# A two-layer hybrid decoder trunk on one core: the order of issue in five places, and a last product in one step

## The chip, the cores and the metric

The kernel runs on one core of one Trainium2 chip. The metric is the device time of one execution in microseconds (us): the median of several runs. A profile is taken of one further execution; its times count from the first instruction of that execution, and its span ends with the last.

## The reference

A trunk of two layers works on x, 512 positions by 1024 channels, in float32. Each layer is half a SwiGLU block (1024 to 2 x 2816, back to 1024), a token mixer, and half a SwiGLU block again, each behind an RMS norm and added to x. The mixer of layer 0 is recurrent, that of layer 1 a gated unit in chunks of 128 positions. A norm with a gain ends it.

```
h = h + 0.5 * swiglu(rms_norm(h, g1), w_in, w_out)
m = recurrent_mixer(hn) or spatial_gating_mixer(hn)
h = h + m
h = h + 0.5 * swiglu(rms_norm(h, g2), w_in, w_out)

recurrent:  y, r = split(hn @ w_in);  r = causal_conv4(r)
            gate_a, gate_x = sigmoid(block_diagonal(r))
            a = exp(-8 * gate_a * softplus(-lam));  b = r * gate_x * sqrt(1 - a*a)
            s[t] = a[t] * s[t-1] + b[t];  m = (gelu(y) * s) @ w_out
gating:     u, v = split(gelu(hn @ w_in));  v = rms_norm(v)
            m = (u * (tril(w_s) @ v + b_s)) @ w_out
```

## The kernel before

All matrix products run on TensorE in the type fp32r with three matmuls for one: an operand is split into a rounded part hi and the rest lo, and hi*hi, lo*hi and hi*lo are summed in one PSUM bank. ScalarE makes hi by a copy, VectorE makes lo by a subtraction (`split`, line 95). Weights are split the same way (whi, wlo, `Sub.split`, line 164). x stays in SBUF for the whole run.

Most products follow a scheme of Strassen's kind: a two by two block product in seven products (`seven`, line 312), named P1, P2, P5, P6, P3, P7, Q4. Their left operands are the quarters A11, A12, A22 and A21 of the activations and the sums S1 to S4 of them; their results are gathered in the PSUM banks A, B, C and, in the output products, Q. A result is put together when the last K slice of a product is done (the functions p1 to q4, the "posts").

The order of all work is written out by hand. `subs` is a list of steps; a step is one weight block (up to 128 x 1024 elements) and the matmuls that use it. The loop at line 1303 walks the list: at step i it runs what was hooked to the step's phase "pre", splits the weights of the steps up to i + 3 (`ahead` sets other numbers for the first steps), runs phase "mid", starts loads, issues the matmuls of step i and with them the posts, and runs the phases "end" and "late". `hook(n, phase, fn)` puts work there. Each engine carries out its instructions in the order of issue, so a hook's place decides what stands behind what on that engine. Weights come through eight raw buffers, loaded on SyncE's queue; accumulating loads go over GpSimd's. There are four buffers each for whi and wlo, so the split for step i + 3 waits for the matmuls of step i - 1. PSUM has six banks for products and two ("aux") for transposes.

The places that the change touches:

- **Opening** (lines 1259 to 1301). The first SwiGLU block begins before the first norm is known: the rows' factor is applied after the product. x is transposed by TensorE in quarters (`turn`), evacuated with the gains by ScalarE (`take`), and the first six steps (`pair_plain`, line 654) use A12, A11, S1 and A22 in two groups of 256 channels. Squares, mean, square root and Newton's step (`squares`, `rstd`) give the rows' factor.
- **Decay constants** (`lru_consts`, line 1152): softplus of lambda on 128 x 8 values, a chain of tiny VectorE operations, drawn at steps 24 to 44 a few at a time.
- **Norm before the recurrent mixer** (`TileNorm`, line 456). For two halves of 256 positions: squares, root, scaled rows xn (`rows`), 16 transposes into four banks (`turn`; two blocks of 128 channels to a bank), and then z as zh (ScalarE) and zl (VectorE) for the eight blocks k = 0 to 7 (`take`). The r and y products sum over these k (`mk`, line 928).
- **Recurrence** (`recurrent`, line 789). Steps 0 to 11 make the eight channel blocks of r: each is evacuated with the first tap of the convolution (rc, ScalarE), gets three more taps (VectorE), is split, goes through the gate matmuls and through two sigmoids and a tanh. Steps 12 to 19 make the eight blocks of y. `plan` (line 902) places for each block the exp and square, oma2 (1 + a squared, times tanh), sqrt, the scan, gelu and the product yh; `drain` moves a y block out of PSUM. The output product begins at step 20.
- **Gating mixer** (`seven_chunk`, line 993): `soon` places gelu and square of v behind the posts p2, p3 and p7.
- **Final norm** (`FinalNorm`, line 730). Tiles 0 and 1 are complete before P7, tiles 2 and 3 with Q4; `mean`, `root`, `newton`, `grown` (times the gain) and `store` write them out.

Of the kernel before, what the change touches and what calls it, by code (L numbers as in the profile page):

```python
# [10 lines left out]
AF = mybir.ActivationFunctionType  # L11
# [5 lines left out]
H = T // 2  # L17
# [16 lines left out]
SLOTS = 60  # L34

# [14 lines left out]
def trunk(ctx: ExitStack, tc: tile.TileContext, a: dict, out: bass.AP):  # L50
# [261 lines left out]
    def seven(block, cuts, left, w, posts, order=None, own=False, apart=False):  # L312
# [4 lines left out]
        bk, raw = {}, {}  # L317
        banks = dict(BANK, Q4=("Q", True)) if apart else BANK

        def mm_of(prod, ci):  # L320
# [3 lines left out]
            def mm(sub):  # L324
                for s in range(2):
                    if fresh and ci == 0:
                        bk[name, s] = bank(name)[:, :w]
                    ps = bk[name, s]
                    k = {} if fresh else dict(skip_group_check=True)
                    for q, i in enumerate(pairs):  # L330
                        zh, zl = left(prod, i, s)
                        wh, wl = sub.hi[:, q, :], sub.lo[:, q, :]
                        end = ci == len(cuts) - 1 and q == len(pairs) - 1
                        nc.tensor.matmul(ps, zh, wh, start=fresh and ci == 0 and q == 0, stop=False, **k)  # L334
# [84 lines left out]
    class BlockNorm:  # L419
# [21 lines left out]
        def rest(self, n, a22=4):  # L441

            for i, g in enumerate(self.g):
                hook(n + (9 if self.plain else a22), "mid", lambda g=g: g.parts("A22"))
# [11 lines left out]
    class TileNorm:  # L456
# [29 lines left out]
        def take(self, half):  # L486
            for k in range(KD):
# [9 lines left out]
        def quarter(self, name):  # L497
            n = now[0]
            last = name == "A21"
            squares(n + 1, "pre" if last else "mid", name)  # L500
            if name == "A12":
                rstd(n, (2, "pre"), (2, "mid"), (3, "pre"), cols=slice(0, 2))
                hook(n + 3, "mid", lambda: self.rows(0))
                hook(n + 3, "end", self.turn)
                hook(n + 4, "mid", lambda: self.take(0))
            elif last:
                S.z = self.z
                rstd(n, (1, "mid"), (1, "mid"), (2, "pre"), cols=slice(2, 4), new=False)
                hook(n + 2, "pre", lambda: self.rows(2))
                hook(n + 2, "end", self.turn)  # L510
                hook(n + 3, "mid", lambda: self.take(1))


    def out_blocks(w, k0, groups, scale, norm=None, order=None, own=False):
# [46 lines left out]
        def q4(s, ps):  # L561
            if hasattr(norm, "last"):
# [7 lines left out]
                      dict(P1=p1, P2=p2, P5=p5, P6=p6, P3=p3, P7=p7, Q4=q4), order, own, True)  # L570
# [83 lines left out]
    def pair_plain(w_in, f0, group, first=False):  # L654
# [24 lines left out]
        def post(half):  # L679
# [6 lines left out]
            left_blocks(group, ht, half, 2)  # L686
# [3 lines left out]
        for h in range(2):  # L690
            subs.append(Sub(raw[0, h], lambda sub, h=h: (product(sub, 0, "A11", h, False, h == 1),
                                                         product(sub, 1, "S1", h, h == 0, False)),
                            None if h == 0 else (lambda: hook(now[0] + 2, "late", lambda: post(0))) if first else
# [36 lines left out]
    class FinalNorm:  # L730
# [40 lines left out]
        def piece(self, t, n):  # L771
            at = now[0]
            hook(at + 1, "mid", lambda: self.mean(t, n))
            if n == 1:
                hook(at + 2, "mid", lambda: self.grown(t, n))
            if t < 2 and n == 1:
# [568 lines left out]
```

## Time and profile before

| what | value |
|---|---|
| median of 3 runs | 1676.83 us (1674.86 to 1677.48) |
| the profiled execution | 1675.16 us, span 1673.5 us |
| TensorE busy | 1627.8 us (97%) |
| VectorE busy | 1374.7 us (82%) |
| ScalarE busy | 1036.1 us (62%) |
| TensorE clock granted, mean | 0.993 of full |

The page gives the busy time of each engine. Further views are used: the waits (who waited for whom: total in us, how often, the longest), windows (for a stretch: length, then busy time and instructions of PE, PEld, DVE, ACT, POOL, then the granted clock of TensorE, the share of the DMA engines and GB/s; a view for one tile shows that tile's instructions alone), and the timeline (start in us, duration in us, engine, line, operation, output <- inputs, shape, how many merged; in brackets the engine's idle time before it and what ended it). PE is TensorE, PEld its weight loads, DVE VectorE, ACT ScalarE, POOL GpSimd, SP SyncE. Of the tiles' names, whi and wlo are split weights, hi and lo split activations, e transposes of activations, p the banks of the first steps, xt and xn those of the norm, r, gate, rc, g, tl, h those of the recurrence, c the parts of v, junk the thrown-away output of a square, ss and ssq its sums, lc the decay constants, raw a weight as loaded.

### The profile page before, as it was taken

How to read it: one execution, taken by the hardware profiler on the slowest of the kernel's cores; microseconds unless marked ns; L12 is line 12 of the kernel's file. 1: busy time of each engine (PE TensorE's matmuls, PEld its weight loads, DVE VectorE, ACT ScalarE, POOL GpSimd, SP SyncE). 2: the span in 40 equal slices, each digit the busy share in tenths (PEclk: the TensorE clock that was granted, in tenths of full speed). 3: DMA queues.
4: the chain of work that ended last, by engine and by line, in shares of the span. 5: the costliest groups of instructions: out<-in, count | busy, mean ns of one | idle time of the engine just before them, and what ended most of it. 6: DMA issues, size and time to landing. Idle time of an engine off the chain costs nothing.

```text
span 1673.5 us, 20804 instructions
## 1 busy us (share of the span) xinstructions
PE 1627.8 (97%) x7477; PEld 1336.2 (80%) x7477; DVE 1374.7 (82%) x1820; ACT 1036.1 (62%) x1487; POOL 210.6 (13%) x191
## 2 busy tenths in 40 slices
PE   7999999989989999999999999999999999999996
PEld 5778888868868878888888788888778887888885
DVE  4898797776698897787888977878965988779778
ACT  6646556666847656556676565566864765565655
POOL 1111111200010111111101111111200011111110
PEclk9999999999999999999999999999999999999998
DMA  6676966952344767876837668768854557686682
GB/s 203 137 174 166 218 161 152 215 150 76 101 106 121 160 176 168 202 171 152 214 119 166 176 162 204 175 154 212 219 159 111 131 124 199 154 211 159 160 208 78
DMA packets 160712, 271.97 MB, mean 163 GB/s; under 512 B 11248, under 2 KB 37472, under 8 KB 160608
## 3 DMA queue, kind: packets, MB, share of 16 engines
q1 hardware_dynamic: 113392, 181.95, 35.3%
q0 software_dynamic: 44992, 86.06, 30.8%
q10 hardware_dynamic: 2224, 2.63, 0.5%
q8 instruction: 59, 0.97, 0.2%
q14 instruction: 45, 0.37, 0.1%
HBM read 268.50 MB, written 2.10 MB: 162 GB/s over the span
## 4 chain that ended last, share of the span: by engine, by line
PE 85%; DVE 9%; ACT 3%; issue 2%; DMA 1%; SPq 0%; ACTq 0%; DVEq 0%
PE A L335 13%; PE A L336 13%; PE A L334 13%; PE C L335 7%; PE C L334 7%; PE C L336 7%; PE e L254 3%; PE B L334 3%; PE B L336 3%; PE B L335 3%; DVE wlo L84 2%; PE p L676 1%; PE p L677 1%; PE p L675 1%; DVE x L90 1%
## 5 line engine op out<-in xcount | busy, mean ns | idle before, releaser
L84 DVE TENSOR_TENSOR wlo<-raw,whi 128x1024 fp32r<-128x1024 f32 (+1 forms) x538 | 640.1, 1192 | 223.8 <-ACT whi L93 223.2
L93 ACT ACTIVATE whi<-raw 128x1024 fp32r<-128x1024 f32 (+1 forms) x538 | 556.1, 1035 | 426.7 <-PE A L335 114.3
L335 PE MATMUL A<-whi,lo 128*128 128x512 f32 x984 | 386.2, 392 | 8.8 <-DVE lo L84 8.6
L334 PE MATMUL A<-whi,hi 128*128 128x512 f32 x984 | 392.4, 399 | 2.1 <-ACT c L93 2.1
L336 PE MATMUL A<-wlo,hi 128*128 128x512 f32 x984 | 384.9, 391 | 0.0
L335 PEld LDWEIGHTS A<-whi,lo 128*128 128x128 f32 x984 | 185.4, 188 | 51.1 <-DVE lo L84 15.1
L336 PEld LDWEIGHTS A<-wlo,hi 128*128 128x128 f32 x984 | 185.2, 188 | 39.9
L334 PEld LDWEIGHTS A<-whi,hi 128*128 128x128 f32 x984 | 185.1, 188 | 39.1 <-ACT c L93 2.6
L335 PE MATMUL C<-whi,lo 128*128 128x512 f32 x544 | 212.3, 390 | 0.7 <-DVE lo L84 0.5
L334 PE MATMUL C<-whi,hi 128*128 128x512 f32 x544 | 212.4, 390 | 0.0
L336 PE MATMUL C<-wlo,hi 128*128 128x512 f32 x544 | 211.8, 389 | 0.0
L131 POOL DMA_DIRECT2D raw<-in_ffn_w_in_dram x80 | 96.4, 1205 | 772.3 <-DVE raw L84 444.9
L84 DVE TENSOR_TENSOR raw<-raw,raw 128x1024 f32<-128x1024 f32 (+1 forms) x118 | 141.5, 1199 | 0.5
L84 DVE TENSOR_TENSOR lo<-a,hi 128x512 fp32r<-128x512 f32 (+1 forms) x196 | 127.2, 658 | 9.5 <-ACT hi L93 9.1
L131 POOL DMA_DIRECT2D raw<-in_ffn_w_out_dram x72 | 83.0, 1153 | 380.2 <-DVE wlo L84 141.3
L93 ACT ACTIVATE hi<-a 128x512 fp32r<-128x512 f32 (+1 forms) x196 | 116.8, 601 | 22.6 <-DVE a L84 20.2
L335 PEld LDWEIGHTS C<-whi,lo 128*128 128x128 f32 x544 | 102.3, 188 | 23.4 <-DVE lo L84 2.2
L336 PEld LDWEIGHTS C<-wlo,hi 128*128 128x128 f32 x544 | 102.3, 188 | 21.2
L334 PEld LDWEIGHTS C<-whi,hi 128*128 128x128 f32 x544 | 102.3, 188 | 21.2
L334 PE MATMUL B<-whi,hi 128*128 128x512 f32 x272 | 109.6, 403 | 0.0
L335 PE MATMUL B<-whi,lo 128*128 128x512 f32 x272 | 106.7, 392 | 1.9 <-DVE lo L84 1.9
L336 PE MATMUL B<-wlo,hi 128*128 128x512 f32 x272 | 106.7, 392 | 0.0
(162 smaller groups left out, 2156.9 us busy)
## 6 DMA issues: line engine op xcount, KB each, us to landing
raw<-in_ffn_w_in_dram SPq DMA_DIRECT2D x160, 512.0 KB, 4.3
raw<-in_ffn_w_out_dram SPq DMA_DIRECT2D x100, 512.0 KB, 5.4
raw<-in_ffn_w_in_dram POOLq DMA_DIRECT2D x80, 512.0 KB, 7.5
raw<-in_ffn_w_out_dram POOLq DMA_DIRECT2D x60, 512.0 KB, 7.8
raw<-in_sg_w_in_dram SPq DMA_DIRECT2D x18, 512.0 KB, 4.8
raw<-in_ffn_w_in_dram SPq DMA_DIRECT2D x32, 256.0 KB, 3.9
raw<-in_rec_w_in_dram SPq DMA_DIRECT2D x16, 512.0 KB, 4.1
raw<-in_ffn_w_out_dram SPq DMA_DIRECT2D x20, 256.0 KB, 4.7
```

The lines of the kernel that those rows point to most:

```text
L84: nc.vector.tensor_tensor(out=o, in0=x, in1=y, op=op)
L90: nc.vector.scalar_tensor_tensor(out=o, in0=x, scalar=s, in1=y, op0=op0, op1=op1)
L93: nc.scalar.activation(out=o, in_=x, func=f, **k)
L131: nc.gpsimd.dma_start(out=self.v, in_=src, accum_op=ALU.add)
L254: nc.tensor.transpose(ps[:, o : o + P], src(q, s), ident)
L334: nc.tensor.matmul(ps, zh, wh, start=fresh and ci == 0 and q == 0, stop=False, **k)
L335: nc.tensor.matmul(ps, zl, wh, start=False, stop=False, **k)
L336: nc.tensor.matmul(ps, zh, wl, start=False, stop=end, **k)
L675: nc.tensor.matmul(ps, zh, wh, start=start and q == 0, stop=False)
L676: nc.tensor.matmul(ps, zl, wh, start=False, stop=False)
L677: nc.tensor.matmul(ps, zh, wl, start=False, stop=stop and q == 1)
```

## The change

The loop gets a phase "rest" between "mid" and the loads. Then:

- Opening: the weights of steps 2 to 6 are split later or in another order; A22 is evacuated by VectorE (`take_plain`) instead of ScalarE; both S1 splits go into step 2's "pre" and both A22 splits into step 3's; the rows' factor is finished at step 4's "pre"; the first gated rows are placed one step earlier for the first half, and their transposes one step later for the second.
- Decay constants: one operation per step, at steps 24 to 100.
- Norm before the recurrent mixer: squares, root, rows and first transposes one phase to one step earlier, a square root of one element to load its table early, and k in the order 0, 2, 4, 6, 1, 3, 5, 7 in `take` and in the products.
- Recurrence: another plan; the exps of blocks 0 to 4 are issued in the step of r block 7, scans from step 14 on instead of 16.
- Gating mixer: gelu and square one to two steps later than before.
- Final norm: other phases; the stores of tiles 0 and 1 at the end; in the last Q4 the matmuls of both K slices are issued together, tile by tile.

```diff
+KORDER = (0, 2, 4, 6, 1, 3, 5, 7)
 def seven(..., joined=None):
             def mm(sub):
+                if prod == joined and ci == 0:
+                    held.extend((sub, q, i) for q, i in enumerate(pairs))
+                    return
                 for s in range(2):
-                    for q, i in enumerate(pairs):
+                    for sb, q, i in (held if prod == joined else []) + [(sub, q, i) for q, i in enumerate(pairs)]:
 class TileNorm, take:
-            for k in range(KD):
+            for k in KORDER:
 class TileNorm, quarter:
-            squares(n + 1, "pre" if last else "mid", name)
+            if name == "A11":
+                hook(n + 4, "rest", lambda: act(tiny(1), ss[:, :1], AF.Sqrt))
+            squares(n + 1, "mid" if name == "A11" else "pre", name)
             if name == "A12":
-                rstd(n, (2, "pre"), (2, "mid"), (3, "pre"), cols=slice(0, 2))
-                hook(n + 3, "mid", lambda: self.rows(0))
-                hook(n + 3, "end", self.turn)
-                hook(n + 4, "mid", lambda: self.take(0))
+                rstd(n, (1, "mid"), (1, "mid"), (2, "pre"), cols=slice(0, 2))
+                hook(n + 2, "mid", lambda: self.rows(0))
+                hook(n + 2, "end", self.turn)
+                hook(n + 3, "mid", lambda: self.take(0))
             elif last:
-                rstd(n, (1, "mid"), (1, "mid"), (2, "pre"), cols=slice(2, 4), new=False)
-                hook(n + 2, "pre", lambda: self.rows(2))
+                rstd(n, (1, "pre"), (1, "pre"), (1, "pre"), cols=slice(2, 4), new=False)
+                hook(n + 1, "pre", lambda: self.rows(2))
                 hook(n + 2, "end", self.turn)
-                hook(n + 3, "mid", lambda: self.take(1))
+                hook(n + 3, "pre", lambda: self.take(1))
 pair_plain:
-            left_blocks(group, ht, half, 2)
+            left_blocks(group, ht, half, 3 if first and half else 2)
-                            (lambda: hook(now[0] + 2, "late", lambda: post(0))) if first else
+                            (lambda: hook(now[0] + 1, "rest", lambda: post(0))) if first else
 class FinalNorm, piece:
+            if t < 2:
+                hook(at + 1, "mid", lambda: self.mean(t, n))
+                if n == 1:
+                    hook(at + 2, "mid", lambda: self.root(t))
+                    hook(at + 3, "mid", lambda: self.newton(t))
+                    hook(at + 3, "rest", lambda: self.grown(t, 1))
+                    hook(at + 4, "late", lambda: self.store(t))
+            else:
+                self.mean(t, n)
+                hook(at + 1, "rest", lambda: self.grown(t, 1))
 class FinalNorm, last:
             stt(xt(t, 0), ps, scale, xt(t, 0), ALU.mult, ALU.add)
+            if t == 3:
+                self.store(2)
             ...
-            self.store(t)
+            if t == 3:
+                self.store(3)
 recurrent:
-        plan(1, "mid", (exp_, 0, 1))
-        plan(2, "mid", (exp_, 2, 3, 4, 5), (drain, 0, 1), (oma2, 0, 1))
-        plan(3, "mid", (exp_, 6, 7), (drain, 2), (oma2, 2, 3, 4, 5, 6, 7), (sqrt, 0, 1))
-        plan(4, "mid", (sqrt, 2, 3, 4, 5, 6, 7), (scan, 0, 1))
-        plan(5, "mid", (gelu, 0, 1, 2, 3, 4), (scan, 2, 3, 4))
-        plan(6, "mid", (gelu, 5), (yh, 0, 1), (scan, 5), (yh, 2, 3), (scan, 6))
-        plan(7, "mid", (gelu, 6), (scan, 7), (yh, 4, 5))
-        hook(y0 + 6, "late", lambda: blk(0, "A11"))
-        hook(y0 + 7, "mid", lambda: blk(0, "A12"))
+        plan(-1, "rest", (exp_, 0, 1, 2, 3, 4))
+        plan(1, "rest", (drain, 0), (oma2, 0, 1, 2, 3, 4), (sqrt, 0, 1, 2, 3, 4))
+        plan(2, "rest", (exp_, 5, 6, 7), (drain, 1), (scan, 0, 1))
+        plan(3, "rest", (drain, 2), (scan, 2, 3))
+        plan(4, "rest", (oma2, 5, 6, 7), (sqrt, 5, 6, 7), (scan, 4))
+        plan(5, "rest", (gelu, 0, 1, 2, 3, 4), (scan, 5, 6))
+        plan(6, "rest", (gelu, 5), (scan, 7), (yh, 0, 1, 2, 3))
+        plan(6, "late", (s1, 0))
+        plan(7, "mid", (gelu, 6), (yh, 4, 5))
+        hook(y0 + 7, "rest", lambda: [blk(0, b) for b in ("A11", "A12", "S1")])
...
-        sums(groups[0], y0 + 9)
+        sums(groups[0], y0 + 8)
 mk (r and y products):
-                    for k in range(KD):
+                    for k in KORDER:
 seven_chunk:
-                hook(now[0] + d, "mid", lambda: done(*args))
+                hook(now[0] + d, "rest", lambda: done(*args))
-                soon(1, s, 0, c1[s], c1[s])
+                soon(2 + s, s, 0, c1[s], c1[s])
-                soon(1, s, 1, c2[s], c2[s])
+                soon(3 + s, s, 1, c2[s], c2[s])
-                soon(2, 2 + s, 1, c5[s], c5[s])
+                soon(2 + s, 2 + s, 1, c5[s], c5[s])
 opening:
-                         (1, "pre", lambda: (take(0, "A11"), take(0, "A22", False))),
-                         (1, "pre", lambda: (take(1, "A11"), take(1, "A22", False))),
+                         (1, "pre", lambda: (take(0, "A11"), take_plain(0, "A22"), take_plain(1, "A22"))),
+                         (1, "pre", lambda: (subs[2].split(), take(1, "A11"))),
-                         (2, "pre", lambda: (take(0, "A21"), take(1, "A21", False))),
-                         (2, "mid", lambda: first.g[1].parts("S1"))):
+                         (2, "pre", lambda: (take(0, "A21", False), take(1, "A21", False))),
+                         (2, "pre", lambda: [g.parts("S1") for g in first.g]),
+                         (3, "pre", lambda: [g.parts("A22") for g in first.g])):
-    rstd(4, (0, "pre"), (0, "mid"), (0, "late"))
+    rstd(3, (0, "late"), (0, "late"), (1, "pre"))
-    for n in range(24, 44):
-        hook(n, "mid", lambda: next(consts, None))
+    for n in range(24, 100):
+        hook(n, "rest", lambda: next(consts, None))
-    ahead = {0: 2, 1: 3, 2: 5}
+    ahead = {0: 1, 1: 3, 2: 4, 3: 6}
```

More of the change, by code (lines that the diff above doesn't have):

```diff
@@ L310, in left_of, with seven @@
         return left
-    def seven(block, cuts, left, w, posts, order=None, own=False, apart=False):
-        bk, raw = {}, {}
+    def seven(block, cuts, left, w, posts, order=None, own=False, apart=False, joined=None):
+        bk, raw, held = {}, {}, []
         banks = dict(BANK, Q4=("Q", True)) if apart else BANK
@@ L443, in rest @@
             for i, g in enumerate(self.g):
-                hook(n + (9 if self.plain else a22), "mid", lambda g=g: g.parts("A22"))
+                if a22 is not None:
+                    hook(n + (9 if self.plain else a22), "mid", lambda g=g: g.parts("A22"))
                 hook(n + 4 + i, "pre", g.s2)
@@ L569, in out_blocks @@
         order = seven(block, cuts, left_of(lambda: [gs[i] for i in range(len(n))]), 512,
-                      dict(P1=p1, P2=p2, P5=p5, P6=p6, P3=p3, P7=p7, Q4=q4), order, own, True)
+                      dict(P1=p1, P2=p2, P5=p5, P6=p6, P3=p3, P7=p7, Q4=q4), order, own, True,
+                      "Q4" if hasattr(norm, "last") else None)
         for i, (prod, ci) in enumerate(order):
@@ L692, in pair_plain @@
                                                          product(sub, 1, "S1", h, h == 0, False)),
-                            None if h == 0 else (lambda: hook(now[0] + 2, "late", lambda: post(0))) if first else
+                            None if h == 0 else (lambda: hook(now[0] + 1, "rest", lambda: post(0))) if first else
                             lambda: post(0)))
@@ L1271, in trunk, with take_plain @@
     opening = {}
+    def take_plain(i, name):
+        g, ps = first.g[i], opening.pop((i, name))
+        t = g.new(name)
+        for q, gain in enumerate(first.src(i, name)[1]):
+            qs = slice(q * H, (q + 1) * H)
+            ts(t[:, qs], ps[:, qs], gain, None, ALU.mult)
     turn(0, "A12")
@@ L1292, in trunk @@
     squares(3, "mid", "A21")
-    rstd(4, (0, "pre"), (0, "mid"), (0, "late"))
-    first.rest(1, 2)
+    rstd(3, (0, "late"), (0, "late"), (1, "pre"))
+    first.rest(1, None)
     hook(20, "end", vec_rest_t)
@@ L1312, in trunk @@
         run("mid")
+        run("rest")
         load_more()
```

46 lines of the change are left out of this document (28 added, 18 removed).

## The prediction

> **What bounds the kernel now.** I read the page first, then who waited for whom on TensorE, then stage windows, then the timelines of ScalarE (ACT) and VectorE (DVE) in five stretches.
>
> ```profile
> span 1673.5 us, 20804 instructions
> PE 1627.8 (97%) x7477; PEld 1336.2 (80%) x7477; DVE 1374.7 (82%) x1820; ACT 1036.1 (62%) x1487; POOL 210.6 (13%) x191
> ```
>
> TensorE (PE) is the bound. The change leaves its products as they are, so it can win only what PE loses to waits and to a lowered clock. Windows of 3.41 us show the clock:
>
> ```profile
> 469.95:473.36 3.41, 1.51 (x7) 0.93 (x5) 3.38 (x8) 2.24 (x4) 0.41 (x1) 1.00 0.38 139
> 476.78:480.19 3.41, 1.51 (x7) 1.07 (x7) 3.41 (x10) 0.70 (x2) 0.00 (x0) 1.00 0.47 86
> 480.19:483.60 3.41, 3.41 (x10) 2.63 (x9) 3.41 (x6) 2.16 (x4) 0.00 (x0) 0.50 0.32 87
> 66.61 0.39 PE L334 MATMUL A<-whi,hi 128*128 128x512 f32 x1
> 67.06 0.39 PE L336 MATMUL A<-wlo,hi 128*128 128x512 f32 x1
> ```
>
> The last two rows are first and third of a run: 0.225 us per matmul. After a window with 1.90 us idle (476.78) the next one was at clock 0.50, half speed, and lost 1.7 us; after another with the same idle (469.95) it was not. So about 1.9 us of idle in one window is where the dip begins, and a dip costs up to 1.7 us. [...]
>
> **The opening (steps 0 to 13).** Step n means what is issued for the n-th weight block.
>
> ```profile
> PE p L675 <- ACT hi L93: 3.8, 3, 1.6
> PE e L254 <- ACT a L93: 3.6, 2, 2.3
> 12.34 1.91 PE L254 MATMUL e<-ident,x 128*128 128x128 f32 x16
> 22.18 0.87 DVE L90 SCALAR_TENSOR_TENSOR s<-e,vec,a 128x256 f32<-128x256 f32 x2
> 28.63 1.22 DVE L84 TENSOR_TENSOR raw<-raw,raw 128x1024 f32<-128x1024 f32 x1
> 31.03 1.23 DVE L84 TENSOR_TENSOR wlo<-raw,whi 128x1024 fp32r<-128x1024 f32 x1 [1.18 <-ACT whi L93]
> 32.17 0.68 DVE L84 TENSOR_TENSOR lo<-s,hi 128x512 fp32r<-128x512 f32 x1
> 26.39 1.06 ACT L93 ACTIVATE whi<-raw 128x1024 fp32r<-128x1024 f32 x1 [2.68 <-DVE raw L84]
> 34.82 0.61 ACT L93 ACTIVATE junk<-x 128x512 f32<-128x512 f32 x1
> 39.37 1.28 ACT L93 ACT_TABLE_LOAD   x1
> 41.71 0.16 DVE L84 TENSOR_TENSOR rt<-rt,ti 128x4 f32<-128x4 f32 x1
> 37.90:66.00 28.10, 25.55 (x114) 20.58 (x115) 27.06 (x44) 20.05 (x32) 4.30 (x4) 1.00 0.45 83
> 63.87 1.21 DVE L84 TENSOR_TENSOR wlo<-raw,whi 128x1024 fp32r<-128x1024 f32 x1
> ```
>
> PE loses 7.4 us in the first two rows, but takes back only what DVE lets it: from 37.9 to 66 DVE is busy 27.06 of 28.10 us. So I follow DVE. Instructions in a row start about 0.09 us before the one ahead ends (31.03 to 32.17 is 1.14).
>
> Now: the first transposes are evacuated and rounded at about 14.3. Then DVE's queue holds lo 0.6, the four plain copies of A22 (new on DVE, off ACT; no row shows one; between 0.16, the tiny row 41.71, and the 0.44 of row 22.18, which reads as many elements of the same kind of bank; I take 0.42 each, 1.7), wlo, lo, wlo, four scaled subtracts 1.75, two lo, two adds: 14.3 + 0.6 + 1.7 + 1.15 + 0.6 + 1.15 + 1.75 + 1.25 + 2.3 is 24.8, with waits for the rounded half about 25.3. The scaled subtracts begin at 19.8 instead of 22.18. From 25.3 ACT is the longest: whi 0.96, four squares with their readouts 2.45, two hi 1.1, two whi 1.9, four squares 2.45, table load and root 1.5, whi 0.96: 36.6. Then DVE's wlo ends at 37.95 with Newton's steps done, where row 41.71 ended at 41.87. Shift: 3.9 us.
>
> From there DVE works on unbroken, so its shift stays. PE gains the shift plus the lead that DVE has where it is least: row 63.87 ends at 65.08 and PE uses it at 67.06: 2.0. Two quarter-size operations (0.34 each) of the later A22/A21 stages move behind this point: 0.7. Together **6.5 us** (3.9 if the lead is not there; at most 9, both wait rows and one dip). Some of the e waits stay, since the A11 copy (ACT) stands behind a rounding that waits for DVE. The weight loads on SP and the accumulating loads on POOL follow the splits, which free their buffers no later than now.
>
> ```profile
> 100.85:117.73 16.88, 3.27 (x19) 1.00 0.79 211
> PE A L335 <- DVE lo L84: 1.1, 2, 0.6
> ```
>
> The first row is the decay constants alone: 19 tiny operations in some 8 steps; the change leaves 8, about 1.9 us less DVE in a stretch where PE waits 1.1 us for lo (0.4 more in product Q). I count **0.9** (0 to 1.5). The rest goes to steps up to 100, where PE never waits.
>
> **Norm before the recurrence.**
>
> ```profile
> 348.26 1.28 DVE L90 SCALAR_TENSOR_TENSOR x<-C,x 128x512 f32<-128x512 f32 x2
> 352.78 0.39 PE L334 MATMUL Q<-whi,hi 128*128 128x512 f32 x1
> 357.99 1.86 PE L482 MATMUL xt<-ident,xn 128*128 128x128 f32 x15 [0.28 <-ACT xn L93]
> 363.22 0.84 ACT L93 ACTIVATE zh<-xt,vec 128x256 fp32r<-128x256 f32 x2 [0.58 <-DVE zl L90]
> 362.43:367.44 5.01, 4.59 (x25) 3.38 (x24) 3.38 (x8) 2.37 (x6) 0.00 (x0) 1.00 0.36 105
> 373.54 0.33 PE L482 MATMUL xt<-ident,xn 128*128 128x128 f32 x1 [3.05 <-ACT xn L93]
> 374.15 3.29 PE L482 MATMUL xt<-ident,xn 128*128 128x128 f32 x15 [0.28 <-ACT xn L93]
> ```
>
> First half: the transposes are asked for a step earlier, when PE is at 352.78. x is there at 349.5; squares (ahead of the split) end at 350.2, whi 351.2, wlo 352.4, lo, mean, root 353.6 (its table already loaded), Newton 354.5, another whi and hi, xn 355.7 and 356.4, DVE's xn 357.2. PE waits about 3 us, and the two Q products end 1.4 later than now. What is queued behind the squares on ACT is the split for two steps on, not yet needed. Then the new order of k helps: in row 363.22 ACT waits 0.58 for DVE's zl of the same bank before each pair; with even blocks first it need not, and the first r block, the stretch 362.43 to 367.44, takes 24 half-width matmuls at 0.12, 2.9, instead of 5.0: minus 2.1. Second half: x at 367.5, squares 368.3, Newton 369.9, xn 370.5 and 371.2; PE is there at 369.6 instead of waiting to 373.54, and the slow transposes (15 in 3.29 at row 374.15 against 1.86 at 357.99, a dip) are gone: the next r block starts at 373.1 instead of 377.1. Sum 4.0, less 0.4 for a likely dip in the first wait: **3.6** (0 to 6).
>
> **Recurrence.**
>
> ```profile
> 425.03 0.78 ACT L93 ACTIVATE rc<-r,vec 128x512 f32<-128x512 f32 x1 [2.79 <-PE r L214]
> 431.63 0.39 PE L212 MATMUL gate<-hi,hi 128*128 128x512 f32 x1
> 434.50:448.29 13.79, 13.79 (x63) 11.41 (x62) 4.25 (x7) 13.54 (x20) 1.20 (x1) 1.00 0.25 78
> 442.09 0.72 ACT L93 ACTIVATE g<-g,lru_nc 128x512 f32<-128x512 f32 x1
> 442.85 0.63 ACT L93 ACTIVATE a<-g 128x512 f32<-128x512 f32 x1
> PE A L335 <- DVE lo L84: 4.7, 2, 2.5
> PE B L335 <- DVE lo L84: 1.9, 1, 1.9
> ```
>
> Five exps with squares (1.28 a pair) are now issued in the step of r block 7, ahead of that block's evacuation rc. ACT is free at 422.2 (425.03 less 2.79): table load 1.3, five pairs 6.4, so rc runs at 429.9 instead of 425.0. Behind it: DVE's three taps (to 432.9), and on ACT a whi, a table load back to sigmoid and block 6's gates (to 434.6), then hi 435.1, lo 435.8. PE wants them at 431.63: **a new wait of 4.2 us**, and a dip of 1.7. [...]
>
> In return DVE begins oma2 at 438 and the scans at 446, inside the stretch 434.50 to 448.29 where it is busy 4.25 of 13.79 us now, and brings A11 and A12 before P1 and P2 want them. The waits of the last two rows (6.6) and two dips (3.3) go; what is late next is lo for the two P6 products, about 1.5 us, since DVE is then unbroken from the scan of block 7 on. Removed 10, added 5.9, the 1.5 partly inside what a dip shifts: **4.0** (a loss of 5.9 if nothing returns; a gain of 10 without the gate wait).
>
> **Gating mixer, first product.**
>
> ```profile
> PE A L334 <- ACT c L93: 2.1, 1, 2.1
> PE A L335 <- DVE lo L84: 0.9, 1, 0.9
> ```
>
> Q4 waits for ACT's copy of P7's bank, which stands behind two gelus and squares. These now come a step or two later, behind the copy: 2.1 and a restart 0.2. The 0.9 was whi behind P2's gelus and their table load; these move back two steps: 0.9. The gelus' readers (v's norm) come ten steps of slack later. **3.2** (2 to 3.5).
>
> **Final norm.**
>
> ```profile
> 1662.33 0.69 DVE L90 SCALAR_TENSOR_TENSOR x<-Q,x 128x512 f32<-128x512 f32 x1
> 1669.34 0.37 ACTq L769 DMA_DIRECT2D out_dram<-x  x1
> ```
>
> Tile 2's last product ends 1.36 us earlier (six matmuls sooner), but DVE is behind: four gain products move ahead of row 1662.33 and two stores behind it; it starts at about 1660.3. The chain of tiles 2 and 3 gains 2 us, then stores of tiles 0 and 1 follow it on ACT and DVE, so the last issue is at about 1669.2: **0.1** (a loss of 1 if four stores at once are slow, a gain of 1.5).
>
> **Sum.** 6.5 + 0.9 + 3.6 + 4.0 + 3.2 + 0.1 = 18.3 us. The profiled execution took 1675.16 (1673.5 of span), the median of three is 1676.83, 1.67 above it: 1656.9 against the profile, 1658.5 against the median.
>
> **Rivals.** *No gate wait* (PE reaches the gate later, or ACT is free sooner): recurrence gains 9.9, in all 24.2: 1652.6. For it: ACT has idle time; against it: in the step in question only 2.8 us. *DVE gives back less*: opening 3.9, norm 1.5, recurrence 0, the others as above: 9.6, 1667.2. For it: 27.06 of 28.10 busy. *The order of k does nothing* (ACT and DVE exclude each other by more than the bank): norm 0, 14.7 in all, 1662.1. *Slower*: DVE's stream alone sets the three stretches and no reorder shortens it. Then the copies cost 1.7 in the opening, the early transposes 1.4, the gate 5.9, against 0.9 and 3.2: 4.9 slower, 1681.7. It decides if DVE's last operations in each stretch come no sooner after its first; against it stands DVE's idle time in 434.50 to 448.29, before the first of PE's waits there.
>
> **Chances.** Forecast 0.44 (its own range 1655 to 1662), no gate wait 0.15, less from DVE 0.25, order of k 0.12, slower 0.04. A measurement of this kernel tells some 0.2% (3.4 us) from no change. Of the DVE case a sixth ends within that: faster 0.92, same 0.04, slower 0.04. The range leaves out half of the DVE case, the slower one and a little of the best: 1651.5 to 1668.
>
> **What would show it.** Right: no wait p <- hi beyond 1 us; a wait gate <- DVE lo of about 4 us and a clock of 0.50 after it; none of A or B on lo over 1 us at P1 and P2; none of A on c in the gating product; r blocks after the norm without waits on zl. Wrong: no gate wait; waits for lo in the second chunk as long as those removed; the last store later than now from PE's end.

## The result and the profile after

The changed kernel takes 1657.75 us (median of 4 runs, 1657.10 to 1658.29); the kernel before, run beside it on the same chip, 1677.15 (1674.86 to 1678.0). The ratio is 0.9886, 95% interval 0.9869 to 0.9903. The forecast was 1658.5.

The head of the page after, against the first fence of the prediction:

```profile
span 1656.6 us, 20803 instructions
PE 1622.6 (98%) x7477; PEld 1333.3 (80%) x7477; DVE 1372.8 (83%) x1824; ACT 1036.0 (63%) x1485; POOL 209.8 (13%) x191
```

The work is the same: DVE and ACT are as busy as before, and PE has as many matmuls. Of the 16.9 us by which the span shrank, 11.7 are time in which PE stood (45.7 us before, 34.0 after). The other 5.2 are busy time of the same matmuls: a row 512 wide takes 0.39 us at full clock and 0.63 at half clock, and just behind a wait 0.50 and 0.80. The waits of PE after that bear on the change (whom it waited for: us in total, times, the longest):

```profile
PE A L343 <- DVE lo L87: 4.2, 10, 0.8
PE gate L215 <- ACT hi L96: 3.6, 1, 3.6
PE xt L491 <- ACT xn L96: 3.1, 2, 2.8
PE e L257 <- ACT a L96: 2.7, 2, 2.0
PE p L688 <- ACT hi L96: 0.5, 1, 0.5
PE A L342 <- ACT c L96: 0.2, 1, 0.2
```

Lines have moved by 3 to 13 (ACT's helper is L96 now, DVE's L87, L90 and L93). A on lo fell from 8.6 to 4.2, p on hi from 3.8 to 0.5, xt on xn from 5.3 to 3.1, A on c from 2.1 to 0.2; B on lo is gone. New is the gate's wait. The places, in PE's timeline after:

```profile
46.98 0.44 PE L257 MATMUL e<-ident,h 128*128 128x128 f32 x2 [2.00 <-ACT a L96]
347.63 0.33 PE L491 MATMUL xt<-ident,xn 128*128 128x128 f32 x1 [2.82 <-ACT xn L96]
422.79 0.80 PE L215 MATMUL gate<-hi,hi 128*128 128x512 f32 x1 [3.63 <-ACT hi L96]
482.51 0.50 PE L343 MATMUL A<-whi,lo 128*128 128x512 f32 x1 [0.80 <-DVE lo L87]
1208.07 0.50 PE L343 MATMUL A<-whi,lo 128*128 128x512 f32 x1 [0.79 <-DVE lo L87]
```

and the windows around the gate's wait and behind it (length; busy us and instructions of PE, PEld, DVE, ACT, POOL; granted clock; DMA share; GB/s):

```profile
417.82:421.24 3.42, 1.34 (x6) 0.76 (x5) 3.05 (x4) 3.39 (x5) 0.00 (x0) 1.00 0.50 91
421.24:424.65 3.41, 1.86 (x4) 1.23 (x5) 2.56 (x4) 2.45 (x4) 0.00 (x0) 0.50 0.46 141
424.65:428.07 3.42, 3.42 (x10) 2.65 (x9) 3.42 (x7) 2.69 (x4) 0.00 (x0) 0.50 0.48 159
433.43:490.00 56.57, 55.74 (x249) 45.59 (x248) 55.75 (x78) 36.25 (x52) 6.01 (x5) 1.00 0.54 122
```

The gate's wait and half clock behind it came as forecast; it is for ACT's hi, where the forecast named DVE's lo, and the half clock (0.50) lasts 6.8 us, where it counted a dip of one window. In the last row DVE is busy 55.75 of 56.57 us: from 433 on it has next to no gap in which to catch up. PE is busy 55.74 us there, so this row alone does not say which of the two sets the end; the experiments have to.

Starts on PE in the two profiled executions (1675.16 and 1658.29 us) give the share of each part. Each row's gain is what the shift grew by since the row above.

| start of | before | after | shift | gain of the part |
|---|---|---|---|---|
| a P1 of the second chunk | 120.21 | 112.06 | 8.15 | opening and constants 8.15 |
| an r block behind the norm | 377.09 | 364.77 | 12.32 | norm 4.2 |
| first p after the recurrence | 522.70 | 507.73 | 14.97 | recurrence 2.65 |
| first u of the gating mixer | 1233.76 | 1216.67 | 17.09 | gating 2.1 |
| end of the span | 1673.5 | 1656.6 | 16.9 | final norm -0.2 |

By the profiles the gain is 16.9 us, by the medians 19.4: the profiled execution of before was among its fastest, that of after the slowest of its four.

### The profile page after: what moved, and what is told of

It reads as the page before. It is cut to its first block, busy times and chain, and to the rows that moved or that the text cites. A ratio compares the mean times of both kernels' runs of the same rounds, so it can differ in the third digit from the quotient of the medians.

```text
span 1656.6 us, 20803 instructions
## 1 busy us (share of the span) xinstructions
PE 1622.6 (98%) x7477; PEld 1333.3 (80%) x7477; DVE 1372.8 (83%) x1824; ACT 1036.0 (63%) x1485; POOL 209.8 (13%) x191
## 4 chain that ended last, share of the span: by engine, by line
PE 88%; DVE 6%; ACT 3%; issue 2%; DMA 0%; SPq 0%; ACTq 0%; DVEq 0%
PE A L343 13%; PE A L344 13%; PE A L342 13%; PE C L343 7%; PE C L344 7%; PE C L342 7%; PE e L257 3%; PE B L342 3%; PE B L344 3%; PE B L343 3%; DVE wlo L87 2%; PE r L215 1%; PE r L216 1%; PE r L217 1%; PE p L690 1%
## 5 line engine op out<-in xcount | busy, mean ns | idle before, releaser
L96 ACT ACTIVATE whi<-raw 128x1024 fp32r<-128x1024 f32 (+1 forms) x538 | 556.1, 1036 | 416.6 <-PE A L343 112.3
L87 DVE TENSOR_TENSOR wlo<-raw,whi 128x1024 fp32r<-128x1024 f32 (+1 forms) x538 | 640.7, 1194 | 206.9 <-ACT whi L96 206.0
L87 DVE TENSOR_TENSOR raw<-raw,raw 128x1024 f32<-128x1024 f32 (+1 forms) x118 | 141.5, 1200 | 0.5
L87 DVE TENSOR_TENSOR lo<-a,hi 128x512 fp32r<-128x512 f32 (+1 forms) x196 | 127.3, 659 | 9.9 <-ACT hi L96 9.5
L96 ACT ACTIVATE hi<-a 128x512 fp32r<-128x512 f32 (+1 forms) x196 | 116.7, 601 | 11.7 <-DVE a L87 9.4
L96 ACT ACTIVATE c<-A 128x512 f32<-128x512 f32 x126 | 73.7, 594 | 52.1 <-PE A L344 51.5
```

Of the source, the lines that this page charges most:

```text
L87: nc.vector.tensor_tensor(out=o, in0=x, in1=y, op=op)
L96: nc.scalar.activation(out=o, in_=x, func=f, **k)
```

## The experiments

Theory 1, the forecast's for the opening: in each stretch the stream of DVE and ACT sets the end, and a wait of PE that is left over is slack. Theory 2, by which the forecast added up the recurrence, the constants and the gating mixer: PE's waits are themselves the loss, and taking one away gives its length. All kernels are the changed one with edits; each of the last three is built on an earlier one. The intervals of the ratios to before (0.003 wide, 5 us) overlap for nearly all of them, mostly through the spread of before; so kernels are compared by their medians of 4 or 5 runs, with the range, and by places in their profiles. They ran on four chips, on which the kernel before had medians from 1675.67 to 1677.89 us; so a difference of less than about 2 us between two medians is not shown by the medians alone. The changed kernel: 1657.75, 1657.10 to 1658.29.

| kernel | median us (range) | ratio to before (95%) |
|---|---|---|
| exps later | 1658.53 (1657.74 to 1659.50) | 0.9889 (0.9874 to 0.9903) |
| gate 7 later | 1659.15 (1659.01 to 1659.45) | 0.9892 (0.9878 to 0.9907) |
| gate 7 later, scans sooner | 1657.44 (1657.05 to 1658.33) | 0.9881 (0.9865 to 0.9898) |
| take first | 1657.48 (1657.30 to 1658.66) | 0.9884 (0.9869 to 0.9898) |
| turn later | 1657.47 (1656.88 to 1659.89) | 0.9889 (0.9875 to 0.9903) |
| k plain | 1661.35 (1660.38 to 1662.24) | 0.9909 (0.9895 to 0.9923) |
| gating old | 1659.88 (1659.22 to 1663.24) | 0.9906 (0.9892 to 0.9920) |
| final norm old | 1657.83 (1657.11 to 1659.32) | 0.9884 (0.9869 to 0.9899) |
| constants old | 1659.62 (1659.35 to 1661.05) | 0.9896 (0.9880 to 0.9913) |
| DVE freed | 1656.36 (1655.13 to 1657.07) | 0.9877 (0.9861 to 0.9893) |
| DVE freed, oma2 sooner | 1655.37 (1653.54 to 1655.83) | 0.9866 (0.9851 to 0.9881) |
| the same, S2 sooner | 1653.82 (1653.42 to 1656.36) | 0.9862 (0.9845 to 0.9878) |

### The gate's wait taken away, in two ways

Exps later:

```diff
-        plan(-1, "rest", (exp_, 0, 1, 2, 3, 4))
+        plan(0, "rest", (exp_, 0, 1, 2, 3, 4))
```

> One line of the planned order: the first five exps with their squares are issued one step later, behind block 7's evacuation and split instead of ahead of them. In both theories the new gate wait (3.63 us before 422.79, PE held from 418.77) and the half clock that follows it (421.24 to 428.07) go, 6.25 us in all. Theory 1, the forecast's: between block 7 and P1 the stream of DVE and ACT sets the end, so what PE does not lose at the gate it loses later. The exps, 6.4 us on ACT, now run behind the evacuation, the square roots end at about 432.5 instead of 431.4, P1 starts between 465.0 and 466.5 and the time is 0 to 1.5 us above the changed kernel: 1657.7 to 1659.3. Theory 2, the rival: what PE waits is what is lost, P1 starts at 458.7 to 459.2 and the time is 1651.5 to 1652.

Gate 7 later:

```diff
-            g = n + (2 if c < 4 else 1)
+            g = n + (2 if c < 4 or c == 7 else 1)
```

> The exps stay where the change put them; instead PE asks for block 7's gate one step later, as for blocks 0 to 3, so that its input is there. The wait before 422.79 and the half clock go, as in the kernel with the exps later. Theory 1 (DVE and ACT set the stretch): block 7's sigmoids move behind the first square roots, which costs ACT one table load more (1.28 us) but its split ahead of 432.34 no longer waits for PE (0.95 us): P1 within 1 us of 465.0, the time 1656.7 to 1658.8. Theory 2 (PE's waits add up): P1 at about 459, the time 1652.

The gate does not wait in either, and neither is faster: by the medians they are 0.8 and 1.4 us slower, and no execution comes near the 1652 of theory 2. PE's timeline and two windows with the exps later:

```profile
459.30 0.50 PE L342 MATMUL A<-whi,hi 128*128 128x512 f32 x1 [0.79 <-ACT hi L96]
464.12 0.80 PE L343 MATMUL A<-whi,lo 128*128 128x512 f32 x1 [4.32 <-DVE lo L87]
```

```profile
412.31:446.76 34.45, 34.45 (x153) 28.53 (x152) 23.29 (x30) 29.00 (x39) 2.41 (x2) 1.00 0.38 96
433.27:490.00 56.73, 51.62 (x222) 41.98 (x221) 56.17 (x78) 36.52 (x53) 6.01 (x5) 0.94 0.55 125
```

P1's first matmul starts early, as theory 2 has it, and its second, the first that needs lo, waits 4.32 us, with half clock behind it. PE stands at P1 now instead of at the gate: from 412.31 to 446.76 it is busy throughout, and DVE, busy 56.17 of 56.73 us from 433.27 on, has not become earlier. With the gate later it is the same wait, with one for hi ahead of it:

```profile
460.69 0.49 PE L342 MATMUL A<-whi,hi 128*128 128x512 f32 x1 [2.00 <-ACT hi L96]
465.50 0.79 PE L343 MATMUL A<-whi,lo 128*128 128x512 f32 x1 [4.32 <-DVE lo L87]
```

Theory 1 holds for the time. Its place for P1 was missed: with the exps later P1 starts at 459.30, about where theory 2 has it, and its second matmul at 464.12, both ahead of the 465.0 to 466.5 expected.

### DVE's order, with the gate later

```diff
-        plan(1, "rest", (drain, 0), (oma2, 0, 1, 2, 3, 4), (sqrt, 0, 1, 2, 3, 4))
-        plan(2, "rest", (exp_, 5, 6, 7), (drain, 1), (scan, 0, 1))
-        plan(3, "rest", (drain, 2), (scan, 2, 3))
+        plan(1, "rest", (drain, 0), (oma2, 0, 1, 2, 3, 4), (sqrt, 0, 1, 2, 3, 4), (scan, 0, 1))
+        plan(2, "rest", (exp_, 5, 6, 7), (drain, 1), (scan, 2, 3))
+        plan(3, "rest", (drain, 2), (scan, 4))
...
```

> As the kernel with the later gate, and every scan is issued one step earlier, so that the first two (pr times tl and the scan, 3.8 us) stand in DVE's queue ahead of the split that DVE waits 4.28 us for before 433.43. Theory 1: that idle time is filled, DVE is through its unbroken work some 3 us earlier, P1 starts at about 462 and the time is 2 to 4 us below the kernel with the later gate alone, 1653.5 to 1656. Theory 2: the order on DVE changes nothing while PE does not wait for it, 0 against the kernel with the later gate alone.

By the medians it is 1.7 us faster than the gate alone. PE's wait for lo at P1 keeps its length, and the one for hi goes from 2.00 to 0.15 us:

```profile
459.66 0.50 PE L342 MATMUL A<-whi,hi 128*128 128x512 f32 x1 [0.15 <-ACT hi L96]
464.48 0.80 PE L343 MATMUL A<-whi,lo 128*128 128x512 f32 x1 [4.32 <-DVE lo L87]
```

P1 starts 1.0 us earlier (460.69 to 459.66) and so does its second matmul (465.50 to 464.48). That is less than expected, because DVE's filled gaps came back in part: it waited 1.65 us before 430.89 and 3.79 before 440.27 for weight splits on ACT, and now waits 1.78 before 441.11 and 1.71 before 454.86.

### Two other waits of PE taken away

Take first, in the opening (hooks of the first pair block's A11 and A12 only):

```diff
-            hook(n + 1, "pre" if first else "mid", lambda: self.take(name, st.pop("ps"), gains))
+            hook(n + 1, "pre" if first or soon else "mid", lambda: self.take(name, st.pop("ps"), gains))
...
```

> In the opening only: ACT copies the first pair block's turned A11 and A12 out of their banks at the head of the step, ahead of the splits and the roundings that wait for DVE's sums, so that PE's two waits of the turned blocks e on ACT's a (2.00 us before 46.98, 0.70 before 50.88) go. Theory 1: from 38 us on DVE works without a break, PE's slack moves to another wait, and the second P6 starts at 59.3 as now or up to 0.6 earlier: 1657.1 to 1657.8. Theory 2: both waits are PE's own loss, P6 2.7 us earlier, 1655.0.

```profile
48.01 0.44 PE L257 MATMUL e<-ident,h 128*128 128x128 f32 x2 [0.28 <-ACT a L96]
51.95 0.50 PE L344 MATMUL C<-wlo,hi 128*128 128x512 f32 x1 [0.27 <-DVE wlo L87]
55.76 0.50 PE L344 MATMUL A<-wlo,hi 128*128 128x512 f32 x1 [0.80 <-DVE wlo L87]
59.63 0.50 PE L344 MATMUL A<-wlo,hi 128*128 128x512 f32 x1 [0.83 <-DVE wlo L87]
```

The 2.70 us on ACT's a are 0.28 now, and 1.90 appear on DVE's split weights. P1 of the second chunk starts at 111.82 instead of 112.06, in a run whose first A was 0.30 earlier already: nothing gained.

Turn later, in the norm:

```diff
-                hook(n + 2, "end", self.turn)
-                hook(n + 3, "mid", lambda: self.take(0))
+                hook(n + 3, "end", self.turn)
+                hook(n + 4, "mid", lambda: self.take(0))
```

> In the norm before the recurrence, the first half's transposes are asked for one product later again, as in the kernel before; all else of the norm stays as the change has it. Both theories: PE's wait for xn (2.82 us before 347.63) shrinks to about 1 us and the half clock after it (349.56 to 352.98, 1.7 us) goes, so PE is through product Q some 3.5 us earlier. Theory 1 (ACT and DVE set the stretch): the first half's rounding comes behind one more weight split on ACT (1.05 us), ends at 357 to 358 as now, and PE waits for it: the r block after the norm and the time within 0.7 us of the changed kernel, 1657.0 to 1658.5. Theory 2 (PE's waits add up): 3.5 us faster, 1654.2.

```profile
354.04 0.39 PE L215 MATMUL r<-zh,whi 128*128 128x256 f32 x1 [1.07 <-ACT zh L96]
355.53 0.58 PE L216 MATMUL r<-zl,whi 128*128 128x256 f32 x1 [1.10 <-DVE zl L93]
```

PE is 3 us sooner at the first r block (354.04 against 357.08) and waits there for ACT and DVE. Behind the second half's transposes the next r block starts at 364.84 against 364.77: the time is the same. Theory 1 holds in both, as for the gate.

### The terms of the sum, each undone

The order of k:

```diff
-KORDER = (0, 2, 4, 6, 1, 3, 5, 7)
+KORDER = tuple(range(8))
```

> The order of k is the plain one again in the first norm's rounding and in the r and y products; nothing else is changed. The forecast: ACT waits again for DVE's readout of the same bank before each pair (0.58 us in the kernel before), the first r block stretches by about 2 us, and since the second half's chain starts behind it, 2 to 3 us are lost: 1659.8 to 1660.8. The rival on record, that the order of k does nothing: 0, within 0.5 us of 1657.75.

It is 3.6 us slower by the medians, 3.4 by the start of the r block behind the norm (368.19 against 364.77); 2 to 3 were expected. ACT's first-half rounding with the plain order (two more rows like the second follow), and its one wait in the changed kernel:

```profile
354.63 0.84 ACT L96 ACTIVATE zh<-xt,vec 128x256 fp32r<-128x256 f32 x2 [1.32 <-DVE zl L93]
356.05 0.84 ACT L96 ACTIVATE zh<-xt,vec 128x256 fp32r<-128x256 f32 x2 [0.58 <-DVE zl L93]
```

```profile
354.28 1.66 ACT L96 ACTIVATE zh<-xt,vec 128x256 fp32r<-128x256 f32 x4 [0.23 <-DVE zl L93]
```

Two neighbours of k lie in one PSUM bank. With the plain order ACT waited before the second of each pair until DVE had read the first, 1.32 us and three times 0.58; with the banks taken in turn one wait of 0.23 us is left. The first r block is not stretched by this: it takes 2.87 us with the plain order (358.43 to 361.30) and 2.88 with the new one (357.08 to 359.96), since the rounding now begins well ahead of it (352.85 and 352.50). The price comes through DVE's queue, where the update of the second half's x stands behind the zl. The first row is the changed kernel's, the second has the plain order:

```profile
358.06 1.28 DVE L93 SCALAR_TENSOR_TENSOR x<-Q,x 128x512 f32<-128x512 f32 x2
361.48 1.28 DVE L93 SCALAR_TENSOR_TENSOR x<-Q,x 128x512 f32<-128x512 f32 x2
```

The second half's squares, root and rows follow 3.4 us later, and PE waits for its xn:

```profile
365.96 0.33 PE L491 MATMUL xt<-ident,xn 128*128 128x128 f32 x1 [1.62 <-ACT xn L96]
```

The gating mixer, with `soon` at "mid" again (that line is not shown) and distances 1, 1, 2 as before:

```diff
...
-                soon(2 + s, s, 0, c1[s], c1[s])
+                soon(1, s, 0, c1[s], c1[s])
...
-                soon(3 + s, s, 1, c2[s], c2[s])
+                soon(1, s, 1, c2[s], c2[s])
...
-                soon(2 + s, 2 + s, 1, c5[s], c5[s])
+                soon(2, 2 + s, 1, c5[s], c5[s])
```

> In the gating mixer's first product, the gelus and their squares stand where the kernel before had them, ahead of ACT's copy of P7's bank and of the splits; all else as changed. Forecast: Q4 waits again for the copy (2.1 and a restart of 0.2) and P6 for lo (0.9): 2 to 3.5 us slower, its value 3.2. By the two profiles, in which this stretch gave 2.2 and a lo wait of 0.79 stayed: 2.2, about 1660. Rival: the stretch that follows is bound by DVE (v's norm, the spatial products), and the earlier gelus let it catch up: under 1 us.

```profile
1195.71 0.50 PE L343 MATMUL A<-whi,lo 128*128 128x512 f32 x1 [0.92 <-DVE lo L87]
1212.04 0.50 PE L342 MATMUL A<-whi,hi 128*128 128x512 f32 x1 [2.14 <-ACT c L96]
```

It is 2.1 us slower by the medians, and the stretch from the first p behind the recurrence to the first u takes 711.0 us instead of 708.9. Both waits are back, but undoing costs only the second, since the changed kernel waits 0.79 for lo elsewhere (row 1208.07 above).

The final norm and the last product in two steps (the code of `piece`, `last` and the call of `seven` as before):

> The end alone undone: the last product in two steps again, and the squares, gains and stores of the final norm ordered as in the kernel before; all else as changed. The forecast's term is 0.1 us for the whole of it (between a loss of 1 and a gain of 1.5): 1657.85, 1656.75 to 1659.25. By the two profiles the end came 0.16 later with the change: 1657.6. Rival: the two steps as one give the 1.36 us of six matmuls by which tile 2's product ends sooner: 1659.1.

0.1 us, no difference. In the changed kernel DVE multiplies four gains before it takes up the last product's first tile, and the last store is issued at 1652.13:

```profile
1640.65 2.49 DVE L87 TENSOR_TENSOR x<-x,fg 128x512 f32<-128x512 f32 x4
1643.06 0.68 DVE L93 SCALAR_TENSOR_TENSOR x<-Q,x 128x512 f32<-128x512 f32 x1
1652.13 0.34 ACTq L782 DMA_DIRECT2D out_dram<-x  x1
```

The same tile and the last store with the old end:

```profile
1644.76 0.69 DVE L93 SCALAR_TENSOR_TENSOR x<-Q,x 128x512 f32<-128x512 f32 x1
1651.76 0.37 ACTq L782 DMA_DIRECT2D out_dram<-x  x1
```

PE's last matmul starts at 1642.51 in the changed kernel and at 1642.03 with the old end. So the tile is taken up 0.55 us behind it instead of 2.73, in spite of the four gains. What this wins is spent at the very end, where the stores of tiles 0 and 1 now follow tile 3: the last store is issued 9.62 us behind PE's last matmul, against 9.73.

The decay constants (`lru_consts` with the yields of before, and the steps):

```diff
-    for n in range(24, 100):
-        hook(n, "rest", lambda: next(consts, None))
-    hook(100, "rest", lambda: list(consts))
+    for n in range(24, 44):
+        hook(n, "mid", lambda: next(consts, None))
+    hook(44, "mid", lambda: list(consts))
```

> The decay constants alone undone: they are computed in steps 24 to 44 again, two and three operations at a time and ahead of each step's weight load requests; all else as changed. The forecast's term is 0.9 us (0 to 1.5): the waits for lo at the second P1 and P2 grow from 0.45 and 0.23 to about 1.1 in all, and 0.4 come back in product Q: 1658.65. Rival: DVE's stream has room there since the opening gave it a lead, 0: 1657.75. The other 7.2 us of the opening's 8.15 are the first product's order of issue, if the term is right.

It is 1.9 us slower by the medians and P1 of the second chunk starts 2.32 later, twice the term. The constants' own operations on DVE from 90 us to 117.7, in this kernel and in the changed one:

```profile
90.00:117.70 27.70, 4.21 (x24) 1.00 0.55 145
```

```profile
90.00:117.70 27.70, 1.68 (x11) 1.00 0.62 166
```

### Kernels that use it

If DVE and ACT set the recurrence's end, work must be taken off DVE, or put into its gaps, ahead of 490. On the exps-later kernel: the scans as above, two `drain` copies on ACT, and A11's rounding ahead of the products yh of blocks 4 and 5:

```diff
-            nc.vector.tensor_copy(y, ym[c])
+            nc.vector.tensor_copy(y, ym[c]) if c == 0 else act(y, ym[c], AF.Copy)
...
+        hook(y0 + 6, "late", lambda: blk(0, "A11"))
...
```

> Built on the kernel with the exps later, whose PE waits only at P1 (0.79 for hi and 4.32 for lo). Added to it: the scans one step earlier, into the 2.73 us for which DVE waits before 433.27; two of the three copies of y out of their banks on ACT instead of DVE (1.2 us less DVE behind 433.27); and block A11's rounding ahead of four small products on DVE. Theory 1: the time follows DVE from 433 on, which is 3.5 to 4 us earlier; 3 to 4.5 us below the kernel with the exps later, 1654 to 1655.5, below both kernels. Theory 2 (PE's waits are the loss, and they stand at P1): A11's earlier rounding alone takes P1's wait away, 5 us, 1653.5. Should DVE's earlier start only move the wait to the splits that PE's steps set free, 0 to 1.5 us.

```profile
476.81 0.47 PE L342 MATMUL A<-whi,hi 128*128 128x512 f32 x1 [0.59 <-DVE x L93]
479.65 0.80 PE L343 MATMUL A<-whi,lo 128*128 128x512 f32 x1 [2.37 <-DVE lo L87]
```

By the medians it is 2.2 us below the kernel it was built on, which is less than expected; in the two profiles the stretch from the last r matmul ahead of gate 7 to the first p shrinks only from 88.60 to 88.14 us. Which of its three edits counted was not taken apart. P1 waits 0.21 for lo and P2 0.63, and the wait has moved to P6, with 6.8 us of half clock from 478.4. Part of the filled gap came back here too: DVE waits 1.72 us before 452.45 for a weight split, behind square roots that wait for oma2. So, next:

```diff
-        plan(3, "rest", (drain, 2), (scan, 4))
-        plan(4, "rest", (oma2, 5, 6, 7), (sqrt, 5, 6, 7), (scan, 5))
+        plan(3, "rest", (drain, 2), (oma2, 5, 6, 7), (scan, 4))
+        plan(4, "rest", (sqrt, 5, 6, 7), (scan, 5))
```

> The kernel with DVE freed, and the last three products of a and tl (oma2 5 to 7, 1.89 us on DVE) one step earlier, so that ACT need not wait 2.13 us for them before its second square roots and the weight split behind these comes earlier; DVE waits 1.72 us for that split before 452.45, the only break in its work up to P6. Theory 1 (the time follows DVE from there): P6's wait (0.59 for x and 2.37 for lo) shrinks by 1.7 us, and with some 1.3 us of idle time left the half clock that follows it there (478.4 to 485.3, 3.4 us of work lost) goes or halves: 2 to 5 us below the kernel with DVE freed, 1651.5 to 1654.5. Rival: the split waits for PE's r step in any case and the break only moves: 0, 1656.4.

```profile
475.09 0.47 PE L342 MATMUL A<-whi,hi 128*128 128x512 f32 x1 [0.24 <-DVE x L93]
477.93 0.50 PE L343 MATMUL A<-whi,lo 128*128 128x512 f32 x1 [2.37 <-DVE lo L87]
```

It is 1.0 us below by the median. DVE's gap before 452 is gone and P6's second matmul starts 1.7 us earlier, so the rival is out. But the wait did not shrink by 1.7: PE came earlier too, and the wait for lo keeps its 2.37 us, since it is DVE's order that makes it: when x is done, PE starts, and DVE has a sum and a weight split to do before lo. Then S2's rounding one step earlier, for the recurrence's P6 alone:

```diff
-                hook(at0 + i - 2, "mid", lambda ci=ci, name=LEFT[prod]: gs[ci].parts(name))
+                hook(at0 + i - (3 if prod == "P6" and getattr(norm, "grow", 0) == V_F2 else 2), "mid", ...)
```

> The last kernel (DVE freed, oma2 earlier) and block S2's rounding for the recurrence's two P6 products one step earlier, so that its lo stands ahead of two updates of x, a sum and a weight split on DVE (3.8 us) instead of behind them. In the last kernel P6 waits 0.24 us for x and 2.61 for lo. Theory 1 in its strict form (DVE is unbroken to 492 us, so only work taken off it counts): the wait moves to the second P6 or to P3, 0 to 0.5 us gained, 1655 to 1655.4. The other reading (behind P6 DVE has room, the product behind the norm shows no wait; what counts is what DVE does ahead of the first thing that PE needs): x comes 0.6 us later, lo is there, 2 us gained, and 1.7 more where the wait had been followed by half clock: 1652 to 1653.5. Either way the fastest of the kernels run here.

```profile
476.18 0.47 PE L342 MATMUL A<-whi,hi 128*128 128x512 f32 x1 [0.84 <-DVE x L93]
479.62 0.33 PE L257 MATMUL e<-ident,x 128*128 128x128 f32 x1 [0.44 <-DVE x L93]
484.88 0.50 PE L343 MATMUL C<-whi,lo 128*128 128x512 f32 x1 [0.69 <-DVE lo L87]
```

The wait for lo at P6 is gone and comes back in pieces. From gate 7 to the first p after the recurrence the kernel without this edit took 84.20 us (418.93 to 503.13) and this one 84.18 (419.42 to 503.60): theory 1 in its strict form. The median is 1.6 us lower, but the ranges overlap; whether it is faster than the last one stays open. By the medians the three kernels built on this are 1.4, 2.4 and 3.9 us below the changed one; their intervals still overlap with its 0.9869 to 0.9903, that of the last only from 0.9869 to 0.9878. In the profiles the stretch from the last r matmul ahead of gate 7 to the first p takes 88.96 us in the changed kernel, 88.14 with DVE freed, and 84.4 in the last two. Of the 4.5 us that these two gain, 3.4 are half clock (6.8 us of it there in the changed kernel, none in these), and about 1.1 is work moved.

## Why the prediction was right, point by point

The time came within 0.8 us, and part of that is luck. The terms miss by up to 1.4 us both ways. By the profiles they come to 16.9 us where the forecast has 18.3, so that the profiled execution, forecast at 1656.9, took 1658.29; by the medians the gain is 19.4. All the signs named for being right came, but for the gate's wait, which is on ACT's hi.

- **What bounds it**: right where it was applied, in the opening, where PE "takes back only what DVE lets it", and the experiments carry it: of the waits of PE that were taken away singly, the gate's (twice) made the kernel 0.8 and 1.4 us slower and those of e and xt 0.3 faster, by the medians; that of lo at P6 gave nothing from gate 7 to the next p, where only its median leaves something open. But the terms for the constants, the recurrence and the gating mixer were added up from PE's waits, and these are the ones that are off by 1.0 to 1.4 us.
- **Opening, 6.5**: about 6.0. The two profiles give 8.15 with the constants; in the kernel with the old constants P1 of the second chunk starts at 114.38, 2.32 later, of which 0.19 were there at the first A: 8.15 - 2.13. The path is the one forecast: DVE's weight split behind ACT's squares ends at 37.45, forecast at 37.95. The wait on a that it left standing costs nothing (take first).
- **Decay constants, 0.9**: 1.9 to 2.1, the term that was sized worst. The step "I count 0.9" took PE's listed waits for the price and one row that begins at 100.85. From 90 on the old order costs DVE 4.21 - 1.68 = 2.5 us more, and with DVE as the bound nearly all of it reaches PE. PE's listed waits for lo came back as forecast (1.1 and 0.4), but by the gaps between its starts it loses 2.0 us more from 72 to 115, in many small waits. That is the forecast's own argument, not applied here.
- **Norm, 3.6**: 4.2 by the profiles, but the step on the order of k failed. Its 2.1 us were to come out of the first r block; that block takes 2.87 or 2.88 us with either order. The order of k is worth 3.4 to 3.6 by another path: DVE is done sooner with the zl and takes up the second half's x sooner (358.06 against 361.48). The early transposes, 1.4 of cost in the forecast and a 0.4 for a dip, cost nothing: undone, the time stays. The rival that the order of k does nothing fell.
- **Recurrence, 4.0**: 2.65 in the profiled executions. Of the difference 0.6 to 1.1 goes with the clock: from gate 7 to the first p it took 84.9 us there, with 6.8 us of half clock, and 83.9 to 84.3 in the kernels take first, turn later, k plain, gating old and constants old, whose recurrence is the same, with 3.4 us. The waits named came (gate 3.63 against 4.2, 0.80 at P6 against 1.5). The step "Removed 10, added 5.9" left out the 1.5 that it names, and counted one dip behind the gate where the profile has 6.8 us of half clock. As a count of what PE lost it nearly holds with the measured sizes (10 less 3.63 and 0.80 of waits and 3.4 for the half clock is 2.2). As a list of prices it was wrong, and with it the rival *no gate wait* at 1652.6: without the wait the time is 1658.5. The gate's wait is not a price of the change. DVE's work from 433 on, and ahead of it the splits that it waits for on ACT (7.34 us before 425.11 with the exps later), set the gain; PE's wait only shows where the slack lies.
- **Gating, 3.2**: 2.1. The wait on c went as forecast (2.1 to 0.2; the restart of 0.2 counted with it was an estimate, and the row behind that wait took 0.50 us against 0.39); the 0.9 for lo at P6 did not: lo is late at P7 instead (0.79 at 1208.07). The step failed that took a removed wait for a gain.
- **Final norm, 0.1**: 0.1 by the medians, -0.2 by the profiles, and by the path forecast. DVE's four gains stand ahead of the last product's tile, the tile is taken up 2.2 us sooner (forecast 2), and the stores of tiles 0 and 1 behind tile 3 take that back.
- **The other rivals**: *DVE gives back less* (3.9, 1.5 and 0 for opening, norm and recurrence) fell, with 6.0, 4.2 and 2.65 measured, and so did *slower*.
- **The table load ahead of the gate**: the forecast counted 1.3 us, from its row 39.37, and the gate's wait was 0.6 shorter than forecast. The two rows of ACT below are in sequence, the load of 1.28 us and the first sigmoid behind it, 1.30 us from start to start:

```profile
419.05 1.28 ACT L96 ACT_TABLE_LOAD   x1
420.35 1.27 ACT L96 ACTIVATE g<-gate,vec 128x512 f32<-128x512 f32 x2
```

## What to carry to other kernels

Where a helper engine is busy nearly all of a stretch (55.75 of 56.57 us here), price an edit by that engine's work and gaps, not by the waits of the engine that you want to feed: here a wait that was taken away came back at the next thing needed. A busy share does not show it alone (PE was as busy there); take one wait away and see. Look for the gaps of the helper ahead of the stretch, and ask of each filled gap what the helper waits for next (here the other helper's weight splits, which took back 3.49 of 5.44 us with the scans sooner and 2.03 of 2.73 with DVE freed). Here ACT waited 1.32 us and three times 0.58 for DVE to read the same PSUM bank, and once 0.23 with the banks taken in turn; that gave 3.6 us for a changed list of eight numbers.

## What the runs showed of the hardware

The same pause of TensorE did not always bring half clock. With DVE freed, PE waited 0.59 and 2.37 us before 476.81 and 479.65, and the clock was 0.51 from 478.4 to 485.3; in the next kernel it waited 0.24 and 2.37 us at the same place, and the clock was 1.00 from 433 to 492. Windows of the second of these kernels, around the wait:

```profile
472.50:475.90 3.40, 2.82 (x12) 1.80 (x10) 3.40 (x5) 2.58 (x4) 1.20 (x1) 1.00 0.00 0
475.90:479.30 3.40, 1.37 (x6) 1.15 (x7) 3.40 (x6) 1.25 (x4) 1.20 (x1) 1.00 0.77 122
479.30:482.70 3.40, 3.35 (x17) 2.53 (x16) 3.40 (x6) 3.40 (x7) 0.00 (x0) 1.00 1.05 181
```

In the changed kernel the half clock behind a pause lasted 3.4 us from 349.56 and 6.8 us from 421.24. There 1.34 us busy in the window that ends where it begins (417.82 to 421.24) went ahead of it, while the 1.37 of the second row above, in a window of nearly the same length, was followed by clock 1.00; what decides between them is not shown. Nor did it take the 1.9 us of idle time that the prediction put as the start of a dip: 1.76 us were enough from 346.15 to 349.56. Half clock is worth up to 1.7 us for 3.4 us of it, an estimate from the granted 0.50: matmuls started 0.43 us apart (424.97 to 427.53), and 0.23 apart behind it (428.25 to 429.87). Executions of one kernel differ in their clock: that of the kernel with oma2 sooner whose windows are above took 1653.54 us at a mean clock of 0.997, the three others 1655.06 to 1655.83 at 0.993 to 0.994.
